# Block sums of the turned rows, made in two halves behind later reciprocal roots: a decoder layer on one core

## The chip, the cores and the metric

The kernel runs on one core of a Trainium2 chip. The metric is the device time of one execution in microseconds (us). The engines are TensorE (PE), VectorE (DVE), ScalarE (ACT), GpSimd (POOL) and SyncE (SP), whose queue issues the DMAs.

## The reference

One layer of a hybrid decoder over a prompt of 2048 rows and 64 sample rows, all in float32 and 1024 wide: input projection, windowed attention and a pooling mixer, an output projection, an MLP of width 4096, and a gate. What matters here stands in the middle:

```
  mix = concat(RMSNorm(attn), RMSNorm(pool)) @ w_out
  x  += RMSNorm(mix)
  x  += RMSNorm(relu(RMSNorm(x) @ w_up)^2 @ w_down)
```

The first row's product and residual, the norm of the new x, and its turning into the operand of `@ w_up` are the place of the change.

## The kernel before, in words

The rows are 16 tiles of 128 (t = 0 to 15) and one of the 64 sample rows (t = -1); two tiles make a pair, pair p having the tiles 2p and 2p + 1. Products are made in three matmuls for accuracy: each operand is split into a rounded half (a cast on ScalarE, L214) and a rest (a subtraction on VectorE, L137).

The stages, by the trace: input projection, attention and pooling until about 425 us; the output mixing until about 600; the up projection until about 1290; the down projection until about 1910; then the gate. The up projection multiplies in blocks of 2 x 2 with seven products instead of eight. Of the turned rows it needs four blocks A11, A12, A21, A22 (the halves of an even tile and of an odd one) as the seven operands A11, A12, A22, S1 to S4, where

    s0 = A21 + A22, s1 = s0 - A11, s2 = A11 - A21, s3 = A12 - s1

are S1 to S4. The kernel writes the operands of every pair to three scratch blocks in DRAM (`hfd`), and the up projection reads them back one block of 352 columns at a time (`sp<-hfd`, L1041; A22 by L1272).

The output mixing goes over the tiles 0, 1, 2, 3, -1, 4, 5 and so on to 13. For a tile:

- `Mixed.product` (L245 to L264) does the products into PSUM (`pab`, L141 to L143) and takes them out: the first half by ScalarE (L260), the second by VectorE with an addition (L262), into `z`.
- `first_residual` (L921 to L932) does the residual: a sum of squares of z on ScalarE (L190, `junk`), a reciprocal root on GpSimd (`rstd_of`: L148 `rst`, then L150 `rsq`), L927 and L928 on VectorE (the new x, stored by L929), a second sum of squares (L190, `z`), a second root, and L931, the normed rows.
- `turned` (L934 to L945) turns the rows of the tile two before: eight transposes on TensorE (L941, `trx`), two copies on ScalarE (L944) into `h`, of which there are three buffers.
- `operands` (L947 to L956) runs behind the odd tile of a pair: four sums by GpSimd (`a_sums`, L898 to L902: L899 s0, L900 s1, L901 s2, L902 s3) into `s`, two buffers; then the stores to `hfd` (L956), from `h` and from `s`.

Pair 7 (tiles 14, 15) is late: its residual and turning run inside the first rounds of the up projection, and `space` makes its operands. Weights of the up projection come in by L1144 (`raw`), are split (`g`), and PSUM is copied out by L1198 (`snap`).

The kernel's instructions are placed by a scheduler that takes each engine's order from the program's order, priorities and its own estimates. `tc.issue_after(x)` tells it to issue what follows on the engine behind x. All loads and stores named here go in one order through SyncE's queue, so one that waits holds all behind it.

Of the kernel before, what the change touches and what calls it, by code (L numbers as in the profile page):

```python
# [14 lines left out]
ALU = mybir.AluOpType  # L15
# [17 lines left out]
NT = SEQ // P  # L33
# [62 lines left out]
def trunk(ctx: ExitStack, tc: tile.TileContext, i: dict, o: dict):  # L96
    nc = tc.nc
    V, A, G, T, SY = nc.vector, nc.scalar, nc.gpsimd, nc.tensor, nc.sync
# [25 lines left out]
    ones, mhalf = small[:, 0:1], small[:, 1:2]  # L124
# [14 lines left out]
    def mm3(ps, lhs, rhs, first, last):  # L139
# [2 lines left out]
        T.matmul(ps, lhs[0], rhs[1], start=False, stop=False)  # L142
        T.matmul(ps, lhs[1], rhs[0], start=False, stop=last)  # L143

    def rstd_of(pool, ss, n, dim, cols=1):

        r = pool.tile([P, cols], F32, tag="rst", bufs=6, name="rst")
        G.tensor_scalar(out=r[:n], in0=ss, scalar1=1.0 / dim, scalar2=EPS, op0=ALU.mult, op1=ALU.add)  # L148
        q = pool.tile([P, cols], F32, tag="rsq", bufs=6, name="rsq")
        G.tensor_tensor(out=q[:n], in0=r[:n], in1=mhalf[:n].to_broadcast([n, cols]) if cols > 1 else mhalf[:n], op=ALU.pow)  # L150
        return q

    def pool(stack, name, bufs=1, **k):
# [5 lines left out]
    class Ring:  # L159
# [11 lines left out]
        def first(self, k):  # L171

            n = len(self.slots)
            self.more(k)
            at = self.n % n
            self.slots, self.n = self.slots[n:] + self.slots[at:n] + self.slots[:at], 0
# [105 lines left out]
    with ExitStack() as sa:  # L282
# [8 lines left out]
        op = sa.enter_context(tc.tile_pool(name="op", bufs=2, space=PSUM, reuse_waits="tile"))  # L291
# [533 lines left out]
        first = front(-1, *heads[-1], res[-1])  # L825
# [5 lines left out]
        for t in range(-1, NT):  # L831
# [8 lines left out]
            p = pooling(t, u, mix, sq)  # L840
# [24 lines left out]
    with ExitStack() as sb:  # L865
# [10 lines left out]
        def pieces(tp):  # L876

            at = tp * P if tp >= 0 else NT // 2 * P
            end, out = at + wid(tp), []
            c = at  # L880
            while c < end:
                n = min(end, (c // UP_N + 1) * UP_N) - c
                out.append((c // UP_N, c % UP_N, c - at, n))
                c += n
            return out
# [9 lines left out]
        pld = {tp: [dp.tile([P, 2, 512], F32, name=f"pld{tp + 1}{k}") for k in range(2)] for tp in range(-1, NT // 2)}  # L895
        zd = {tp: dp.tile([P, 2, D], F32, name=f"zd{tp}") for tp in SPILLED}

        def a_sums(eng, s, a11, a12, a21, a22):  # L898
            eng.tensor_tensor(out=s[:, 0], in0=a21, in1=a22, op=ALU.add)  # L899
            eng.tensor_tensor(out=s[:, 1], in0=s[:, 0], in1=a11, op=ALU.subtract)  # L900
            eng.tensor_tensor(out=s[:, 2], in0=a11, in1=a21, op=ALU.subtract)  # L901
            eng.tensor_tensor(out=s[:, 3], in0=a12, in1=s[:, 1], op=ALU.subtract)  # L902

# [1 line left out]
        with s2:  # L907
            p2 = pool(s2r, "p2", side="right")
            gpost, gmlp = rows_of(p2, "g_post_mix"), rows_of(p2, "g_pre_mlp")

            def mix_out(t, nh):
                if t not in mixed.z:
                    mixed.z[t] = p2.tile([P, D], F32, tag="z", bufs=2, name="z")
                    mixed.load(t)
                for _ in mixed.product(t, nh, acc, p2):
                    pass

            added = {}

            def first_residual(t):  # L920

                n = tn(t)
                z = mixed.z[t]
                xt = p2.tile([P, D], F32, tag="xt", bufs=2, name="xt")
                SY.dma_start(xt[:n], xrows(t))
                rs = sumsq(p2, z[:n], n, p2.tile([P, D], BF16, tag="junk", bufs=1, name="junk"))
                V.scalar_tensor_tensor(out=z[:n], in0=z[:n], scalar=rs[:n], in1=gpost[:n], op0=ALU.mult, op1=ALU.mult)  # L927
                added[t] = V.tensor_tensor(out=xt[:n], in0=xt[:n], in1=z[:n], op=ALU.add)  # L928
                SY.dma_start(x1d[t][:n], xt[:n])  # L929
                rs = sumsq(p2, xt[:n], n, z)  # L930
                V.scalar_tensor_tensor(out=z[:n], in0=xt[:n], scalar=rs[:n], in1=gmlp[:n], op0=ALU.mult, op1=ALU.mult)  # L931
                return z  # L932

            def turned(t, z, after=False):  # L934

                n = tn(t)
                h8 = p2.tile([P, 8, P], F32, tag="h", bufs=3, name="h")
                for j in range(2):
                    ps = trb.tile([P, 4, P], F32, tag="tr", name="trx")
                    for c in range(4):  # L940
                        m = T.transpose(ps[:, c, :n], z[:n, (4 * j + c) * P : (4 * j + c + 1) * P], ident[:n, :n])  # L941
                        if after and c == 0:
                            tc.keep_in_program_order(m)
                    A.copy(out=h8[:, 4 * j : 4 * j + 4, :n], in_=ps[:, :, :n])  # L944
                return h8  # L945

            def operands(tp, a, b):  # L947

                n = wid(tp)
                (a11, a12), (a21, a22) = halves(a), halves(b)  # L950
                s = p2.tile([P, 4, 4, P], F32, tag="s", bufs=2, name="s")[:, :, :, :n]
                a_sums(G, s, a11, a12, a21, a22)
                for blk, off, c0, m in pieces(tp):
                    for k, src in ((A11, a), (A22, a22), (S1, s.rearrange("p s c n -> p (s c) n"))):
                        dst = hfd[blk][:, k : k + src.shape[1] // 4, :, off : off + m].rearrange("p o c n -> p (o c) n")
                        SY.dma_start(dst, src[:, :, c0 : c0 + m])  # L956

            h8 = {}

            def turn(t):  # L960

                h8[t] = turned(t, normed.pop(t), True)
                if t < 0:
                    operands(-1, h8[t][:, :, : NS // 2], h8[t][:, :, NS // 2 : NS])
                elif t % 2:
                    operands(t // 2, h8[t - 1], h8[t])

            normed, due = {}, []
            for tp in [0, 1, -1, 2, 3, 4, 5, 6]:
                for t in pairs_of(tp):  # L970
                    if tp:
                        mix_out(t, 0)
                        mix_out(t, 1)
                        if len(due) > 1 or due[0] > 1:
                            turn(due.pop(0))
                    normed[t] = first_residual(t)
                    due.append(t)


            late = list(pairs_of(NT // 2 - 1))  # L980
            for nh in range(2):
                for t in late:
                    mix_out(t, nh)
                    while due:
                        turn(due.pop(0))
            late_h = []

            def turn_late():
                t = late[len(late_h)]
                late_h.append(turned(t, normed[t], True))  # L990

            def residual_late(k):
                normed[late[k]] = first_residual(late[k])
# [22 lines left out]
        with ExitStack() as s3:  # L1016
# [32 lines left out]

            def space():  # L1050

                operands(NT // 2 - 1, *late_h)
                s2r.close()
                for n in ("x0", "x1"):
                    ops[n] = Ring(s3, n, 1)
                g3.first(3)
# [912 lines left out]
```

## Time and profile before

| | us |
|---|---|
| median of 3 runs | 2132.93 |
| the runs | 2132.93, 2133.65, 2127.79 |
| profiled execution, its own time | 2133.05 |
| span of the profiled execution | 2131.2 |
| granted TensorE clock, mean | 0.996 |

The span is from the first instruction to the last; 1.85 us of the time lie around it. In rows of the timeline the first number is the start in us, the second the duration in us, then engine, line, operation, output <- input, shapes, and in brackets how long the engine was idle before and what ended it. The four sums of a pair on GpSimd, in one view that groups the rows of 420 to 640 us by line (pair -1's smaller ones among them, "+1 forms"):

```profile
L901 POOL TENSOR_TENSOR s<-h 128x512 f32<-128x512 f32 (+1 forms) x9 | 17.0, 1890 | 13.5 <-ACT h L944 13.5
L900 POOL TENSOR_TENSOR s<-s,h 128x512 f32<-128x512 f32 (+1 forms) x9 | 16.9, 1879 | 0.7
L899 POOL TENSOR_TENSOR s<-h 128x512 f32<-128x512 f32 (+1 forms) x9 | 16.8, 1872 | 0.6 <-ACT h L944 0.6
L902 POOL TENSOR_TENSOR s<-h,s 128x512 f32<-128x512 f32 (+1 forms) x9 | 11.9, 1326 | 0.6
```

Behind the bar stand the busy time, the mean ns of one, and the idle time of GpSimd just before them with what ended it: 62.6 us of sums in all.

### The profile page before, as it was taken

How to read it: one execution, taken by the hardware profiler on the slowest of the kernel's cores; microseconds unless marked ns; L12 is line 12 of the kernel's file. 1: busy time of each engine (PE TensorE's matmuls, PEld its weight loads, DVE VectorE, ACT ScalarE, POOL GpSimd, SP SyncE). 2: the span in 40 equal slices, each digit the busy share in tenths (PEclk: the TensorE clock that was granted, in tenths of full speed). 3: DMA queues.
4: the chain of work that ended last, by engine and by line, in shares of the span. 5: the costliest groups of instructions: out<-in, count | busy, mean ns of one | idle time of the engine just before them, and what ended most of it. 6: DMA issues, size and time to landing. Idle time of an engine off the chain costs nothing.

```text
span 2131.2 us, 31320 instructions
## 1 busy us (share of the span) xinstructions
PE 2099.9 (99%) x11223; PEld 1851.0 (87%) x11223; DVE 1609.5 (76%) x2749; ACT 1029.7 (48%) x2018; POOL 646.9 (30%) x689
## 2 busy tenths in 40 slices
PE   9999999999999999999999999999999999999999
PEld 7888888788789999999999998888888888887787
DVE  6888988776689888655654567778888888896786
ACT  4667676645455456454544445523323323333553
POOL 1434444354441110000000004643443443432242
PEclk9999999999999999999999999999999999999999
DMA  7453322768789989986767663223123123248563
GB/s 221 147 175 97 93 63 91 268 217 248 226 252 320 310 288 348 273 246 204 233 207 217 213 191 113 80 93 121 51 92 100 51 92 101 90 159 333 187 196 121
DMA packets 334250, 379.76 MB, mean 178 GB/s; under 512 B 82511, under 2 KB 263951, under 8 KB 323822
## 3 DMA queue, kind: packets, MB, share of 16 engines
q1 hardware_dynamic: 334094, 377.76, 55.5%
q8 instruction: 88, 1.44, 0.3%
q14 instruction: 68, 0.56, 0.1%
HBM read 247.90 MB, written 131.09 MB: 178 GB/s over the span
## 4 chain that ended last, share of the span: by engine, by line
PE 78%; DMA 6%; DVE 6%; issue 4%; POOL 3%; ACT 2%; SPq 1%; DVEq 0%; ACTq 0%; POOLq 0%
PE dn L1483 10%; PE dn L1485 10%; PE dn L1484 10%; PE up L1191 9%; PE up L1193 9%; PE up L1192 9%; PE pg L1720 2%; PE pg L1722 2%; PE pg L1721 2%; PE trp L584 1%; PE qps L141 1%; PE qps L143 1%; PE qps L142 1%; DMA x<-in_x_prompt_dram 1%; DMA xt<-in_x_t_dram 1%
## 5 line engine op out<-in xcount | busy, mean ns | idle before, releaser
L1493 DVE TENSOR_TENSOR z<-dn,z 128x512 f32<-128x512 f32 x416 | 280.0, 685 | 91.5 <-PE dn L1485 85.3
L137 DVE TENSOR_TENSOR g<-raw,g 128x512 fp32r<-128x512 f32 x336 | 233.6, 713 | 98.6 <-ACT g L214 91.1
L1191 PE MATMUL up<-e,g 128*128 128x352 f32 x832 | 268.4, 324 | 5.1 <-ACT snap L1198 4.7
L1192 PE MATMUL up<-e,g 128*128 128x352 f32 x832 | 268.0, 322 | 0.0
L1193 PE MATMUL up<-e,g 128*128 128x352 f32 x832 | 265.0, 323 | 0.0
L214 ACT CAST g<-raw 128x512 fp32r<-128x512 f32 x336 | 203.4, 622 | 87.0 <-PE up L1193 64.6
L1432 POOL TENSOR_TENSOR raws<-raws 128x1024 f32<-128x1024 f32 x32 | 80.3, 2511 | 429.0 <-DMA raws<-in_w_down_dram 376.0
L1483 PE MATMUL dn<-wr,ms 128*128 128x512 f32 x512 | 199.4, 390 | 0.0
L1484 PE MATMUL dn<-wr,ms 128*128 128x512 f32 x512 | 199.2, 389 | 0.0
L1485 PE MATMUL dn<-wr,ms 128*128 128x512 f32 x512 | 198.0, 389 | 0.0
L1191 PEld LDWEIGHTS up<-e,g 128*128 128x128 f32 x832 | 156.6, 188 | 6.9 <-ACT snap L1198 5.3
L1192 PEld LDWEIGHTS up<-e,g 128*128 128x128 f32 x832 | 157.3, 189 | 0.7
L1193 PEld LDWEIGHTS up<-e,g 128*128 128x128 f32 x832 | 156.1, 188 | 0.0
L214 ACT CAST m<-fr 128x512 fp32r<-128x512 f32 (+1 forms) x128 | 65.4, 515 | 182.5 <-PE dn L1485 156.6
L899 POOL TENSOR_TENSOR s<-fr 128x256 f32<-128x256 f32 x64 | 49.1, 767 | 332.2 <-DVE ms L137 241.8
L1483 PE MATMUL dn<-wr,m 128*128 128x512 f32 x384 | 149.7, 390 | 0.0
L1484 PE MATMUL dn<-wr,m 128*128 128x512 f32 x384 | 149.4, 389 | 0.0
L1485 PE MATMUL dn<-wr,m 128*128 128x512 f32 x384 | 149.4, 389 | 0.0
L1205 DVE TENSOR_TENSOR t<-up,snap 128x352 f32<-128x352 f32 x144 | 71.3, 520 | 77.3 <-ACT snap L1198 66.1
L1198 ACT COPY snap<-up 128x352 f32<-128x352 f32 x144 | 62.2, 454 | 136.8 <-PE up L1193 136.8
L1483 PEld LDWEIGHTS dn<-wr,ms 128*128 128x128 f32 x512 | 96.1, 188 | 20.4 <-DVE z L1493 0.4
L1485 PEld LDWEIGHTS dn<-wr,ms 128*128 128x128 f32 x512 | 96.1, 188 | 20.0
(398 smaller groups left out, 5772.9 us busy)
## 6 DMA issues: line engine op xcount, KB each, us to landing
raw<-in_w_up_dram SPq DMA_DIRECT2D x160, 256.0 KB, 4.9
raw<-upt SPq DMA_DIRECT2D x32, 1024.0 KB, 8.0
fr<-ffd SPq DMA_DIRECT2D x64, 512.0 KB, 3.6
ffd<-r SPq DMA_DIRECT2D x96, 256.0 KB, 3.0
upt<-raw SPq DMA_DIRECT2D x16, 1024.0 KB, 5.8
raws<-in_w_down_dram SPq DMA_DIRECT2D x32, 512.0 KB, 5.3
sp<-hfd SPq DMA_DIRECT2D x21, 704.0 KB, 5.6
gwd<-gw SPq DMA_DIRECT2D x28, 512.0 KB, 5.9
```

What stands on the lines that cost most here:

```text
L137: eng.tensor_tensor(out=out, in0=full, in1=hi.bitcast(F32), op=ALU.subtract)
L214: copy(out=dst[:, 0], in_=src)
L1191: T.matmul(ps, l[0], r[0], start=st, stop=False, skip_group_check=not fresh)
L1192: T.matmul(ps, l[0], r[1], start=False, stop=False, skip_group_check=not fresh)
L1193: T.matmul(ps, l[1], r[0], start=False, stop=c == 3, skip_group_check=not fresh)
L1198: snapped.append(A.copy(out=s, in_=ps))
L1205: V.tensor_tensor(out=t, in0=ps, in1=s, op=ALU.add)
L1432: tc.keep_in_program_order(G.tensor_tensor(out=t, in0=x, in1=y, op=ALU.subtract))
L1483: T.matmul(ps, l[0], r[0], start=fresh and j == 0, stop=False, skip_group_check=not fresh)
L1484: T.matmul(ps, l[0], r[1], start=False, stop=False, skip_group_check=not fresh)
L1485: T.matmul(ps, l[1], r[0], start=False, stop=j == 1, skip_group_check=not fresh)
L1493: V.tensor_tensor(out=z, in0=ps, in1=z, op=ALU.add)
```

## The change

`rstd_of` remembers its latest root in `rooted`. `a_sums` takes a part: 0 makes s0 and s2, 1 makes s1 and s3, none all four. `operands` stores A11, A12 and A22 at once and puts the two halves of the sums into a list; the second half also stores S1 to S4. A new `gap`, called at the end of each `first_residual`, takes one half off the list and issues it behind the latest root, which is that tile's second. So a pair's halves lie behind the second roots of two successive tiles. For pair 7, `space` empties the list at once.

```diff
+    rooted = [None]
...
-        G.tensor_tensor(out=q[:n], in0=r[:n], in1=mhalf[:n].to_broadcast([n, cols]) if cols > 1 else mhalf[:n], op=ALU.pow)
+        rooted[0] = G.tensor_tensor(out=q[:n], in0=r[:n], in1=mhalf[:n].to_broadcast([n, cols]) if cols > 1 else mhalf[:n], op=ALU.pow)
...
-        def a_sums(eng, s, a11, a12, a21, a22):
-            eng.tensor_tensor(out=s[:, 0], in0=a21, in1=a22, op=ALU.add)
-            eng.tensor_tensor(out=s[:, 1], in0=s[:, 0], in1=a11, op=ALU.subtract)
-            eng.tensor_tensor(out=s[:, 2], in0=a11, in1=a21, op=ALU.subtract)
-            eng.tensor_tensor(out=s[:, 3], in0=a12, in1=s[:, 1], op=ALU.subtract)
+        def a_sums(eng, s, a11, a12, a21, a22, part=None):
+            if part != 1:
+                eng.tensor_tensor(out=s[:, 0], in0=a21, in1=a22, op=ALU.add)
+                eng.tensor_tensor(out=s[:, 2], in0=a11, in1=a21, op=ALU.subtract)
+            if part != 0:
+                eng.tensor_tensor(out=s[:, 1], in0=s[:, 0], in1=a11, op=ALU.subtract)
+                eng.tensor_tensor(out=s[:, 3], in0=a12, in1=s[:, 1], op=ALU.subtract)
...
                 V.scalar_tensor_tensor(out=z[:n], in0=xt[:n], scalar=rs[:n], in1=gmlp[:n], op0=ALU.mult, op1=ALU.mult)
+                gap()
                 return z
...
-                a_sums(G, s, a11, a12, a21, a22)
-                for blk, off, c0, m in pieces(tp):
-                    for k, src in ((A11, a), (A22, a22), (S1, s.rearrange("p s c n -> p (s c) n"))):
-                        dst = hfd[blk][:, k : k + src.shape[1] // 4, :, off : off + m].rearrange("p o c n -> p (o c) n")
-                        SY.dma_start(dst, src[:, :, c0 : c0 + m])
+
+                def store(*srcs):
+                    for blk, off, c0, m in pieces(tp):
+                        for k, src in srcs:
+                            dst = hfd[blk][:, k : k + src.shape[1] // 4, :, off : off + m].rearrange("p o c n -> p (o c) n")
+                            SY.dma_start(dst, src[:, :, c0 : c0 + m])
+
+                def first():
+                    a_sums(G, s, a11, a12, a21, a22, 0)
+
+                def second():
+                    a_sums(G, s, a11, a12, a21, a22, 1)
+                    store((S1, s.rearrange("p s c n -> p (s c) n")))
+
+                store((A11, a), (A22, a22))
+                sums.extend((first, second))
+                if now:
+                    while sums:
+                        sums.pop(0)()
+
+            sums = []
+
+            def gap():
+
+                if sums:
+                    with tc.issue_after(rooted[0].ins):
+                        sums.pop(0)()
...
-                operands(NT // 2 - 1, *late_h)
+                operands(NT // 2 - 1, *late_h, now=True)
```

The lines of the changed kernel are numbered two higher from L143 on, and more behind `a_sums`: L150 and L152 are the root, L902, L903, L905, L906 are s0, s2, s1, s3, L949 the copies to `h`, L962 the stores to `hfd`, L1068 the operand loads, L1171 the weights, L1225 `snap`.

**GpSimd, the sums of pair 3** (tiles 6 and 7; `s_6237` before, `s_6233` after). Before, from the second root of tile 8:

```order
L150 TENSOR_TENSOR rsq_6159<-rst_6157,small_69 128x1
L901 TENSOR_TENSOR s_6237<-h_6130,h_6224 128x512
L899 TENSOR_TENSOR s_6237<-h_6224 128x512
L900 TENSOR_TENSOR s_6237<-s_6237,h_6130 128x512
L148 TENSOR_SCALAR rst_6250<-ss_6248 128x1
L902 TENSOR_TENSOR s_6237<-h_6130,s_6237 128x512
L150 TENSOR_TENSOR rsq_6252<-rst_6250,small_69 128x1
```

Now, from the second root of tile 10:

```order
L152 TENSOR_TENSOR rsq_6350<-rst_6348,small_69 128x1
L902 TENSOR_TENSOR s_6233<-h_6220 128x512
L903 TENSOR_TENSOR s_6233<-h_6124,h_6220 128x512
L150 TENSOR_SCALAR rst_6438<-ss_6436 128x1
L152 TENSOR_TENSOR rsq_6440<-rst_6438,small_69 128x1
L150 TENSOR_SCALAR rst_6447<-ss_6445 128x1
L152 TENSOR_TENSOR rsq_6449<-rst_6447,small_69 128x1
L905 TENSOR_TENSOR s_6233<-s_6233,h_6124 128x512
L906 TENSOR_TENSOR s_6233<-h_6124,s_6233 128x512
```

The four sums, which stood around tile 9's first root, are now two behind tile 10's second root and two behind tile 11's.

**ScalarE, the end of the mixing and the entry of the up projection.** `z_6659` is tile 14's z before, `z_6653` now; `junk_7080` and `junk_7071` are tile 15's first sum of squares; `l0` is the cast of S4. Before:

```order
L944 COPY h_6706<-trx_6707 128x512
L260 ACTIVATE z_6727<-pab_6733,rap_67 128x512
L260 ACTIVATE z_6727<-pab_6789,rap_67 128x512
L944 COPY h_6706<-trx_6713 128x512
L190 ACTIVATE z_6659,ss_7015<-xt_7003 128x1024
L214 CAST l0_6944<-sp_6942 128x1408
L190 ACTIVATE junk_7080,ss_7081<-z_6727 128x1024
L1198 COPY snap_6968<-up_6955 128x352
```

Now:

```order
L262 ACTIVATE z_6716<-pab_6722,rap_67 128x512
L262 ACTIVATE z_6716<-pab_6778,rap_67 128x512
L192 ACTIVATE z_6653,ss_7004<-xt_6992 128x1024
L192 ACTIVATE junk_7071,ss_7072<-z_6716 128x1024
L216 CAST l0_6933<-sp_6931 128x1408
L1225 COPY snap_6957<-up_6944 128x352
L216 CAST l1_6975<-sp_6936 128x1408
L216 CAST g3_7018<-raw_6939 128x512
L949 COPY h_6700<-trx_6701 128x512
L949 COPY h_6700<-trx_6707 128x512
```

Tile 13's copies to `h` stood around the two L260; they are now behind the first `snap`. Tile 15's junk is now ahead of the cast of S4.

**SyncE, the same place.** `sp_6942` before and `sp_6931` now are the load of S4 for the up projection's first block. Before:

```order
L956 DMA hfd1_5253<-s_6629 128x16x64
L956 DMA hfd2_5254<-s_6629 128x16x64
L956 DMA hfd2_5254<-h_6693 128x8x128
L929 DMA x1d14_5294<-xt_6640 128x1024
L1144 DMA raw_7098<-in_w_up_dram 128x4x128 x2
L925 DMA xt_7078<-in_x_prompt_dram 128x1024
L1144 DMA raw_7098<-in_w_up_dram 128x4x128 x2
L1041 DMA sp_6942<-hfd0_5252 128x1408
```

Now:

```order
L933 DMA x1d14_5294<-xt_6631 128x1024
L929 DMA xt_7069<-in_x_prompt_dram 128x1024
L962 DMA hfd1_5253<-s_6430 128x16x128
L962 DMA hfd2_5254<-h_6687 128x8x128
L1171 DMA raw_7093<-in_w_up_dram 128x4x128 x4
L1068 DMA sp_6931<-hfd0_5252 128x1408
```

Ahead of the weights and the load of S4 stood the sums of pair 5 (`s_6629`); now those of pair 4 (`s_6430`) stand there, and pair 5's store has gone into the up projection, ahead of the weights of its fourth round.

More of the change, by code (lines that the diff above doesn't have):

```diff
@@ L945, in turned, with operands @@
                 return h8
-            def operands(tp, a, b):
+            def operands(tp, a, b, now=False):
                 n = wid(tp)
```

## The prediction

> **What bounds the kernel now.** I read the page first: busy times, then the costliest groups.
>
> ```profile
> PE 2099.9 (99%) x11223; PEld 1851.0 (87%) x11223; DVE 1609.5 (76%) x2749; ACT 1029.7 (48%) x2018; POOL 646.9 (30%) x689
> L1191 PE MATMUL up<-e,g 128*128 128x352 f32 x832 | 268.4, 324 | 5.1 <-ACT snap L1198 4.7
> ```
>
> TensorE is busy for 2099.9 of 2131.2 us. The change takes no matmul away, so all it can give back is time in which TensorE waits or runs slowly near the moved sums. The first sum is made soon after 420 us and the last before 640; so the second view is TensorE's own waits from 420 to 700 us.
>
> ```profile
> PE up L1191 <- ACT snap L1198: 4.1, 1, 4.1
> PE pab L141 <- ACT z L260: 1.3, 1, 1.3
> PE up L1191 <- ACT g L214: 0.4, 1, 0.4
> ```
>
> Columns: total us, times, longest. Two waits matter. The timeline of TensorE has them (start, duration, and in brackets the idle time before):
>
> ```profile
> 567.96 0.39 PE L143 MATMUL pab<-wo,ms 128*128 128x512 f32 x1
> 569.69 0.50 PE L141 MATMUL pab<-wo,ms 128*128 128x512 f32 x1 [1.34 <-ACT z L260]
> ...
> 605.60 0.32 PE L1193 MATMUL up<-e,g 128*128 128x352 f32 x1
> 610.07 0.43 PE L1191 MATMUL up<-e,g 128*128 128x352 f32 x1 [4.14 <-ACT snap L1198]
> ...
> 610.74 0.50 PE L1191 MATMUL up<-e,g 128*128 128x352 f32 x1
> 611.03 0.50 PE L1192 MATMUL up<-e,g 128*128 128x352 f32 x1
> ```
>
> The first is inside the output mixing (L141 to L143): start to start 1.73 us where a matmul takes about 0.23, so 1.5 lost. The second is at the entry of the up projection: 4.47 from start to start, 4.3 lost. Behind it 11 matmuls start 0.29 apart (610.74 to 611.03) where I count 0.16 before and after: another 11 x 0.13 = 1.5 us at a lower clock. With two smaller gaps of about 0.5 us together that I found between matmul starts, and 0.4 from the table, the sum of everything the change could win is 1.5 + 4.3 + 1.5 + 0.5 + 0.4 = 8.2 us, 0.4% of the run. That is the first bound.
>
> A rule of the Trainium skill bears on the slow matmuls: "TensorE: Matmul & The Clock Gate", Part 1, says that an idle window of some 3.4 us halves the clock until the engine has been busy for as long. The trace agrees in part: the 4.14 us wait is followed by about 3 us at 0.29 against 0.16. By this rule the 1.5 us go as soon as the wait falls clearly below 3.4 us; my forecast does not need it.
>
> **Why the sums could matter at all: the loop of the residual.** Each tile of the mixing has two sums of squares; GpSimd makes a reciprocal root of each (L148, L150), VectorE then scales (L927, L931), corrects the next operand (L137) and adds the next products (L262), after which ScalarE's next sum of squares (L190) starts the next tile. So first root to first root is the length of one turn. GpSimd's timeline, a pair with its four block sums:
>
> ```profile
> 487.48 0.19 POOL L148 TENSOR_SCALAR rst<-ss 128x1 f32<-128x1 f32 x1 [0.59 <-ACT junk L190]
> ...
> 498.15 0.19 POOL L148 TENSOR_SCALAR rst<-ss 128x1 f32<-128x1 f32 x1 [5.11 <-ACT junk L190]
> ...
> 523.25 0.25 POOL L148 TENSOR_SCALAR rst<-ss 128x1 f32<-128x1 f32 x1 [5.11 <-ACT junk L190]
> ...
> 529.46 1.89 POOL L901 TENSOR_TENSOR s<-h 128x512 f32<-128x512 f32 x1 [0.59 <-ACT h L944]
> 531.30 2.28 POOL L899 TENSOR_TENSOR s<-h 128x512 f32<-128x512 f32 x1
> 533.66 2.77 POOL L900 TENSOR_TENSOR s<-s,h 128x512 f32<-128x512 f32 x1
> 536.51 0.19 POOL L148 TENSOR_SCALAR rst<-ss 128x1 f32<-128x1 f32 x1
> 536.78 1.29 POOL L902 TENSOR_TENSOR s<-h,s 128x512 f32<-128x512 f32 x1
> ...
> 548.51 0.25 POOL L148 TENSOR_SCALAR rst<-ss 128x1 f32<-128x1 f32 x1 [5.11 <-ACT junk L190]
> ```
>
> A turn without a sum takes 498.15 - 487.48 = 10.67 us. With sums 536.51 - 523.25 = 13.26, then 548.51 - 536.51 = 12.00: 12.63 on the mean. TensorE's own pace comes from the grouped rows of 60 us without a wait:
>
> ```profile
> L141 PE MATMUL pab<-wo,ms 128*128 128x512 f32 x82 | 32.5, 396 | 0.0
> L941 PE MATMUL trx<-ident,z 128*128 128x128 f32 x40 | 5.2, 272 | 0.0
> ```
>
> 82 of L141 in 60 us, and 16 to a tile: 60 x 16 / 82 = 11.7 us a tile. The loop with sums (12.63) is 0.9 slower than TensorE, the loop without (10.67) faster by 1.0; TensorE begins with a lead and uses it up at about 544 us, and only then waits. That is the 1.5 us at 568.
>
> **What the change does to the loop.** It adds and removes no instruction on GpSimd: two sums behind the second root of each of two tiles instead of four in a row behind the turned odd tile. Two effects oppose each other.
>
> *Gain.* L900 stands no more ahead of a first root (533.66 to 536.43, the root at 536.51), nor L902 between the two halves of one (1.29 us). The dear turn loses up to 13.26 - 12.00 = 1.3 us, so 0.6 us a tile at most if the cheap one stays as it is.
>
> *Loss.* VectorE's L931 waits for that same second root, so the sums now start at the same moment as L931 and L137, on every tile. What that does is in VectorE's rows beside a pair's sums and away from them:
>
> ```profile
> 599.66 2.31 DVE L927 SCALAR_TENSOR_TENSOR z<-z,rsq,g_post_mix 128x1024 f32<-128x1024 f32 x1 [2.19 <-POOL rsq L150]
> 602.00 2.20 DVE L928 TENSOR_TENSOR xt<-xt,z 128x1024 f32<-128x1024 f32 x1
> ...
> 612.45 1.27 DVE L927 SCALAR_TENSOR_TENSOR z<-z,rsq,g_post_mix 128x1024 f32<-128x1024 f32 x1
> ```
>
> ```profile
> 591.92 2.33 POOL L148 TENSOR_SCALAR rst<-ss 128x1 f32<-128x1 f32 x1 [4.45 <-ACT z L190]
> ...
> 599.59 1.30 POOL L901 TENSOR_TENSOR s<-h 128x512 f32<-128x512 f32 x1
> 600.91 2.21 POOL L899 TENSOR_TENSOR s<-h 128x512 f32<-128x512 f32 x1
> ```
>
> The same L927 takes 2.31 where a sum started 0.07 us earlier, and 1.27 alone; the second sum takes 2.21 instead of 1.30. They take turns. Placed behind the second root: sum one 0 to 1.3 us, L931 done at 2.3 (instead of 1.3), sum two to 3.5, L137 to 4.6 (instead of 2.5), the two L262 to 6.0. So the path is longer by up to 2 us than the turn without a sum: 10.67 + 2.0 = 12.7 us, on every tile. Against 12.63 that is nothing. If VectorE went first, the turn would be about 1 us shorter, 11.7, which is TensorE's own pace.
>
> The Trainium skill's "SBUF — State Buffer", section on the two separate sides, says that VectorE operations with two SBUF inputs and GpSimd share a port pair under an exclusive lock, and that whoever starts first keeps it for the whole instruction. The rows above agree (2.31 against 1.27). By the rule the order of arrival decides, and it speaks against this change: GpSimd, whose own root has just ended, would arrive first.
>
> The h copies (L944) come into this too. Their buffers (three) come free only behind the sums, which are now behind the previous tile's second root. ScalarE therefore makes them behind the products' copies L260, as the rows in the section on the change show. That takes the first half's copy (about 0.6 us) out of the way of L260, for which TensorE waited at 569.69; at 3.5 us behind the root the sums end before L262 does (6.0), so the copies hide beside VectorE. I take the mixing as even: bounds are -2.0 us (1.5 and the small gaps vanish) and, if every turn costs the dear 13.26, (13.26 - 12.63) x 9 tiles with full sums = +5.7.
>
> **The entry of the up projection.** ScalarE's rows:
>
> ```profile
> 604.30 1.06 ACT L190 ACTIVATE z<-xt 128x1024 f32<-128x1024 f32 x1 [3.46 <-DVE xt L928]
> ...
> 607.26 1.37 ACT L214 CAST l<-sp 128x1408 fp32r<-128x1408 f32 x1 [1.81 <-DMA sp<-hfd]
> 608.53 1.05 ACT L190 ACTIVATE junk<-z 128x1024 bf16<-128x1024 f32 x1
> ...
> 609.58 0.43 ACT L1198 COPY snap<-up 128x352 f32<-128x352 f32 x1
> ```
>
> The copy of PSUM (L1198) that TensorE waits for since 605.9 stands behind the cast l, and that behind a DMA of the operand S4. In the changed order the 1.05 us of junk stand ahead of the cast, in time spent waiting for the DMA: if the DMA lands at 607.2 as before, the copy comes at 608.5, a gain of 1.05. What sets the landing is on SyncE's queue:
>
> ```profile
> 586.99 1.59 SPq L956 DMA_DIRECT2D hfd<-s  x2
> ...
> 596.84 0.93 SPq L1144 DMA_DIRECT2D raw<-in_w_up_dram  x2
> ...
> 599.43 0.46 SPq L1041 DMA_DIRECT2D sp<-hfd  x1
> ```
>
> The load stands behind four weight loads (raw), which wait for VectorE's last L137 on the previous weights. Two things come new ahead of it. The S store of 1 MB for pair 4 (s_6430 in the order) waits for the second half of its sums behind tile 13's second root: its L148 ends at 594.25 above (591.92 + 2.33, held up beside VectorE), plus 2.6 for two sums alone, 3.5 beside VectorE, so 597 to 598. And VectorE's L137 contend with these sums. So S4 leaves at 599 to 601 and lands, with 1 MB more ahead of it, up to 3.3 us later. The price of 1 MB is from the windows (DMA share and GB/s last):
>
> ```profile
> 570.00:600.00 30.00, 29.98 (x144) 24.70 (x143) 19.25 (x22) 16.55 (x31) 12.88 (x15) 1.00 0.66 169
> 600.00:612.00 12.00, 7.86 (x45) 7.57 (x44) 8.83 (x8) 6.53 (x10) 8.34 (x8) 0.94 0.96 302
> 612.00:640.00 28.00, 28.00 (x176) 27.96 (x175) 25.43 (x36) 15.18 (x31) 10.44 (x6) 0.96 0.83 261
> 640.00:700.00 60.00, 59.55 (x371) 58.94 (x370) 56.28 (x92) 32.25 (x62) 6.31 (x4) 1.00 1.01 325
> ```
>
> At 302 GB/s 1 MB is 3.5 us. From zero to 3.5 late against 1.05 gained: -1 to +2.5, and below that -5.8 (4.3 + 1.5) if S4 is early because the raw weights come free earlier. I take -0.5, near the end with no delay, since the 30 us ahead move only 169 GB/s and have room for a store.
>
> Later stores: pair 5's 1 MB of S goes from 587 into the time behind tile 15's second root, about 624. There the DMA engines have a few idle microseconds (the window from 612 to 640 has a share of 0.83); from 640 on they are full (1.01), and a store that is not done by then costs up to 3.3 us (1 MB at 325 GB/s) of the weight stream. The weights have some slack behind 630, so I take nothing. Everything after the up projection's first block has the same order on all engines: nothing.
>
> **Sum.** Mixing 0, entry -0.5, later 0: about 2132.5 from the profiled 2133.05 (span 2131.2 plus 1.85 around it). The median of the runs, 2132.93, is 0.1 below that, so the forecast on its scale is **2132**.
>
> **Rivals.** (1) *The loop falls to TensorE's pace.* VectorE gets its turn first, the turns are 11.7, TensorE reaches the entry late by nothing, z(14) is early since pair 6's sums no longer stand beside L927 and L928 (2.31 and 2.20 instead of 1.27), and S4 with it: -2.0 - 5.8 = -7.8 at most, 2125; half of it 2129. For it: GpSimd is idle for 5.11 us ahead of the first roots. Against: the sums start at the root, not in that idle time, and S4 does not hang on z(14). (2) *Every turn becomes a dear one*, because sum two, the late S3 cast's L137 (in one tile between L931 and the next) and the h copies follow one another on every tile: +5.7, plus a slow entry with 1 to 2.5: 2139 to 2141. Decides from turns of 13.2 us on. For it: the port is shared at the worst place. Against: first roots are no longer held by L900. (3) *S4 lands late*, mixing even: +2.5 to +3.3, 2135 to 2136. That the sums are not moved at all is excluded by the order itself.
>
> **How the numbers follow.** About even, 2130 to 2135: 0.50. Rival 1: 0.22, half of it with over 6.4 us. Rival 2: 0.16. Rival 3: 0.12. A measurement of this kernel can tell about 0.3% (6.4 us) from no change; the three runs before lie 5.9 apart. Faster by more: 0.11; slower by more: 0.17 (rival 2 and a little of rival 3); within: 0.72. The range runs from 2126 to 2140: rival 1 but for its best end, rival 2's nearer part.
>
> **What would show it.** Turns between first roots of 12.5 to 12.9 on all tiles, instead of 13.2 and 12.0 in turn, would show the loop right; L931 at 2.3 and L137 at about 2.2 beside a sum would show the contention. The wait at the entry should stay between 3 and 5.5 us with the slow matmuls behind it. The forecast is wrong if turns are 11.7 or below, if the cast l starts before 605 or after 610, or if TensorE gets waits of over 1 us between 612 and 700.

## The result, and the profile after

The changed kernel takes **2147.41 us** (median of 6 runs, 2142.76 to 2151.55) against 2131.29 (6 runs, 2127.79 to 2133.65): slower, ratio 1.0076, 95% interval 1.0064 to 1.0089. The forecast was 2132 with a range to 2140. The profiled execution is the fastest of the six: 2142.76, span 2141.0, 9.8 us above the span before. Of the 16 us between the medians the two profiles show 10: the profiled execution before is 1.8 above its median, and the changed kernel's median is 4.7 above its profiled one. What slower executions lose more is in no profile; a second profile of the same kernel, further down, has a time of 2144.32.

TensorE's work is nearly the same. The page's first line and the group that carried the wait before:

```profile
PE 2105.1 (98%) x11223; PEld 1855.3 (87%) x11223; DVE 1626.1 (76%) x2749; ACT 1032.4 (48%) x2018; POOL 641.7 (30%) x689
L1218 PE MATMUL up<-e,g 128*128 128x352 f32 x832 | 268.5, 324 | 3.9 <-ACT snap L1225 3.9
```

What grew is TensorE's waits from 420 to 760 us (total, times, longest):

```profile
PE pab L141 <- ACT z L262: 5.3, 2, 4.6
PE up L1218 <- ACT snap L1225: 4.8, 2, 3.4
PE pab L143 <- DVE ms L137: 2.5, 1, 2.5
PE up L1220 <- DVE g L137: 2.0, 2, 1.4
```

They add up to 14.6 us, against 7.0 before in the same window (the waits shown ahead and one of 1.0 for snap behind 700). The wait in the mixing (the first and third row) has gone from 1.3 to 7.8; the entry's wait for snap has fallen from 4.1 to 3.4, and 2.0 for weights are new. The timeline of TensorE has the two in the mixing:

```profile
566.25 0.39 PE L143 MATMUL pab<-wo,ms 128*128 128x512 f32 x1
571.22 0.80 PE L141 MATMUL pab<-wo,ms 128*128 128x512 f32 x1 [4.59 <-ACT z L262]
...
586.24 0.39 PE L142 MATMUL pab<-wo,ms 128*128 128x512 f32 x1
589.10 0.50 PE L143 MATMUL pab<-wo,ms 128*128 128x512 f32 x1 [2.47 <-DVE ms L137]
```

Behind the first, matmuls start 0.43 apart instead of 0.23 until 576.5 (granted clock 0.50 from 573 to 576), which is 2.5 us more; behind the second wait it is about 1.1. The 1.5 us of slow matmuls behind the entry are still there, 0.29 apart from 617.8 to 620.8. So there are 7.6 more of waits and 3.6 more of slow matmuls.

The rows of TensorE can also be counted by stage, since both traces have all of them. From the first to the last of the 800 matmuls of the mixing's products (`pab`) it is 204.4 us before and 214.7 now, so the mixing takes 10.3 more. The first 200 matmuls of the up projection take 39.7 and 41.7. From the first product of the mixing to the end of the span it is 12.0 more; the spans differ by less, 9.8, because this execution came to the mixing 2.3 us earlier.

**The loop did what the prediction worked out, and one thing more.** GpSimd's timeline of the changed kernel (first roots are the rst that a junk released):

```profile
535.61 0.19 POOL L150 TENSOR_SCALAR rst<-ss 128x1 f32<-128x1 f32 x1 [3.68 <-ACT junk L192]
...
541.08 1.29 POOL L905 TENSOR_TENSOR s<-s,h 128x512 f32<-128x512 f32 x1
542.45 2.16 POOL L906 TENSOR_TENSOR s<-h,s 128x512 f32<-128x512 f32 x1
548.28 0.19 POOL L150 TENSOR_SCALAR rst<-ss 128x1 f32<-128x1 f32 x1 [3.68 <-ACT junk L192]
...
561.91 0.57 POOL L150 TENSOR_SCALAR rst<-ss 128x1 f32<-128x1 f32 x1 [4.56 <-ACT junk L192]
...
576.45 0.19 POOL L150 TENSOR_SCALAR rst<-ss 128x1 f32<-128x1 f32 x1 [5.21 <-ACT junk L192]
...
584.47 1.29 POOL L902 TENSOR_TENSOR s<-h 128x512 f32<-128x512 f32 x1
...
591.64 0.19 POOL L150 TENSOR_SCALAR rst<-ss 128x1 f32<-128x1 f32 x1 [3.67 <-ACT junk L192]
```

548.28 - 535.61 = 12.67 us for a turn, as worked out; the one before it took 13.05. The next three are 13.63, 14.54 and 15.19. Why they grow stands in ScalarE's and VectorE's rows:

```profile
568.27 1.37 ACT L216 CAST e<-sp 128x1408 fp32r<-128x1408 f32 x1 [1.39 <-DMA sp<-hfd]
569.54 1.04 ACT L216 CAST ms<-mr 128x1024 fp32r<-128x1024 f32 x1
570.49 1.26 ACT L262 ACTIVATE z<-pab,rap 128x512 f32<-128x512 f32 x2
...
580.78 1.38 ACT L216 CAST e<-sp 128x1408 fp32r<-128x1408 f32 x1 [4.42 <-DMA sp<-hfd]
582.07 1.05 ACT L192 ACTIVATE z<-xt 128x1024 f32<-128x1024 f32 x1
```

```profile
567.83 2.28 DVE L935 SCALAR_TENSOR_TENSOR z<-xt,rsq,g_pre_mlp 128x1024 f32<-128x1024 f32 x1 [2.14 <-POOL rsq L152]
570.03 2.69 DVE L137 TENSOR_TENSOR e<-sp,e 128x1408 fp32r<-128x1408 f32 x1
572.64 1.22 DVE L137 TENSOR_TENSOR ms<-mr,ms 128x1024 fp32r<-128x1024 f32 x1
...
584.54 2.30 DVE L935 SCALAR_TENSOR_TENSOR z<-xt,rsq,g_pre_mlp 128x1024 f32<-128x1024 f32 x1 [0.72 <-POOL rsq L152]
586.77 2.28 DVE L137 TENSOR_TENSOR ms<-mr,ms 128x1024 fp32r<-128x1024 f32 x1
```

The casts e are the S operands of the up projection's first block, S3 at 568.27 and S1 at 580.78. ScalarE does its work in order, so while it waits for their DMA everything behind it waits: at 568.27 the cast of ms and the L262 for which TensorE stands still, at 580.78 the second sum of squares of the loop. The second wait, for ms, ends with L137 at 589.05: that L137 and the L935 ahead of it run beside sums of pair 4 and take 2.3 each.

The loads are late because a store of the sums is, and because they follow one another through one buffer. SyncE's queue:

```profile
544.64 3.08 SPq L962 DMA_DIRECT2D hfd<-s  x2
...
551.38 0.52 SPq L1068 DMA_DIRECT2D sp<-hfd  x1
...
562.46 0.32 SPq L1068 DMA_DIRECT2D sp<-hfd  x1
...
571.26 0.37 SPq L962 DMA_DIRECT2D hfd<-s  x1
572.75 1.77 SPq L1068 DMA_DIRECT2D sp<-hfd  x1
```

The store at 544.64 is that of pair 2's sums, part of which the first block reads. Behind it S2's load leaves at 551.38, where it left at 523.48 before. S3's load leaves when VectorE has ended with S2's rest, at 562.46. The load of S1 stands behind the store of pair 3's sums, which before was issued at 538.10, but what it waits for last is the buffer: it leaves at 572.75, as soon as VectorE has ended with S3's rest (570.03 + 2.69), and lands eight us later.

The collision itself, in groups of VectorE from 420 to 600 us, L931 before and L935 now:

```profile
L931 DVE SCALAR_TENSOR_TENSOR z<-xt,rsq,g_pre_mlp 128x1024 f32<-128x1024 f32 (+1 forms) x13 | 17.7, 1363 | 19.2 <-ACT ms L214 15.6 <-POOL rsq L150 3.7
```

```profile
L935 DVE SCALAR_TENSOR_TENSOR z<-xt,rsq,g_pre_mlp 128x1024 f32<-128x1024 f32 (+1 forms) x13 | 27.3, 2099 | 19.3 <-ACT ms L216 10.8 <-POOL rsq L152 8.4
```

17.7 has become 27.3 us for the same 13 instructions. The rule of the Trainium skill ("SBUF — State Buffer", the section on the two separate sides) that the prediction weighed, that whoever comes first keeps the shared ports for the whole instruction, is what the rows of the changed kernel show: GpSimd's first sum takes 1.29, L935 beside it 2.3.

### The profile page after: what moved, and what is told of

The parts are those of the page before. It is cut to its first block, busy times and chain, and to the rows that moved or that the text cites. A ratio compares the mean times of both kernels' runs of the same rounds, so it can differ in the third digit from the quotient of the medians.

```text
span 2141.0 us, 31293 instructions
## 1 busy us (share of the span) xinstructions
PE 2105.1 (98%) x11223; PEld 1855.3 (87%) x11223; DVE 1626.1 (76%) x2749; ACT 1032.4 (48%) x2018; POOL 641.7 (30%) x689
## 4 chain that ended last, share of the span: by engine, by line
PE 75%; DMA 7%; DVE 6%; issue 6%; POOL 3%; ACT 2%; SPq 1%; DVEq 0%; ACTq 0%; POOLq 0%
PE dn L1510 9%; PE dn L1512 9%; PE dn L1511 9%; PE up L1220 8%; PE up L1218 8%; PE up L1219 8%; PE pg L1747 2%; PE pg L1749 2%; PE pg L1748 2%; DMA gwd<-gw 1%; PE trp L586 1%; DMA wod<-wsp 1%; PE qps L141 1%; PE qps L143 1%; PE qps L142 1%
## 5 line engine op out<-in xcount | busy, mean ns | idle before, releaser
L137 DVE TENSOR_TENSOR g<-raw,g 128x512 fp32r<-128x512 f32 x336 | 241.4, 738 | 91.0 <-ACT g L216 84.9
L902 POOL TENSOR_TENSOR s<-fr 128x256 f32<-128x256 f32 x64 | 49.1, 767 | 332.7 <-DVE ms L137 245.5
L1225 ACT COPY snap<-up 128x352 f32<-128x352 f32 x144 | 62.2, 455 | 129.7 <-PE up L1220 129.7
```

The source lines that it names most:

```text
L137: eng.tensor_tensor(out=out, in0=full, in1=hi.bitcast(F32), op=ALU.subtract)
L1225: snapped.append(A.copy(out=s, in_=ps))
```

## The experiments

All are shown against runs of the kernel before on the same chip.

| run | halves behind second roots | median us | ratio, 95% interval |
|---|---|---|---|
| the change | up to pair 5; pair 6 when `space` empties the list | 2147.41 | 1.0076 [1.0064, 1.0089] |
| e1 | pairs 3 to 6 | 2138.59 | 1.0035 [1.0022, 1.0048] |
| e2 | 0 to 2, the rest at once | 2134.11 | 1.0015 [1.0006, 1.0025] |
| e3 | as the change, casts of S2, S3, S1 later | 2145.24 | 1.0064 [1.0049, 1.0079] |
| e4 | as the change, behind VectorE's L137 up to tile 12 | 2131.64 | 1.0000 [0.9990, 1.0010] |
| e5 | pairs 3 and 4 | 2131.85 | 1.0014 [1.0005, 1.0023] |
| e6 | pairs 0 to 4 | 2138.27 | 1.0040 [1.0025, 1.0054] |
| e7 | none | 2130.16 | 1.0002 [0.9992, 1.0011] |
| e8 | as e4, a tile earlier | 2140.60 | 1.0052 [1.0037, 1.0067] |
| e9 | as e8, pairs 0 to 4 | 2138.22 | 1.0036 [1.0024, 1.0047] |
| e10 | kernel before, snap ahead of S4's cast | 2133.45 | 1.0011 [1.0001, 1.0020] |
| e11 | e9 and e10 together | 2140.28 | 1.0049 [1.0030, 1.0068] |
| e12 | the change again | 2145.63 | 1.0070 [1.0049, 1.0092] |
| e13 | pairs 5 and 6 as in the change, the rest at once | 2139.43 | 1.0051 [1.0034, 1.0068] |
| e14 | 0 to 2 exactly as in the change | 2138.10 | 1.0052 [1.0034, 1.0071] |
| e15 | as e14, behind L137 | 2135.42 | 1.0025 [1.0015, 1.0035] |

The edits move the scheduler's order on other engines, too, so a run is never one price alone. Each run has one profile, of one execution.

**e1: pairs 0 to 2 at once.**

```diff
-                if now:
+                if now or tp < 3:
```

> Only pairs 3 to 5 have their halves behind the second roots; pairs 0, 1, -1 and 2, which make up the first block of the up projection, have them at once as before. Theory A (the late S operands of the first block: their casts stand in ScalarE's and VectorE's order ahead of the residual's steps and wait for DMA, which holds the mixing at 566 to 593 us): the loss goes, 2128 to 2135 us, no TensorE wait over 2 us between 540 and 600. Theory B (sums and VectorE colliding behind every second root): tiles 10 to 13 still collide, 2138 to 2145.

Measured 2138.59, by the time in theory B's range. But in the mixing theory A holds: no wait over 0.8 us from 540 to 600, where the change has 7.1. The time is not back, since two waits of 4.8 us stand behind it, one of them new, in the up projection:

```profile
638.72 0.52 PE L1218 MATMUL up<-l,g 128*128 128x352 f32 x1 [4.73 <-DVE t L1232]
```

GpSimd runs eight sums on end there, pair 6's and pair 7's:

```profile
624.37 1.29 POOL L902 TENSOR_TENSOR s<-h 128x512 f32<-128x512 f32 x1
...
636.25 1.59 POOL L906 TENSOR_TENSOR s<-h,s 128x512 f32<-128x512 f32 x1
```

So there are two places, not one. (The list is shorter in this run, so it is pair 6 and not pair 5 that the gap behind tile 15's root took. The expectation counts pair -1 to the first block; its 32 columns are in the third, by `pieces`.)

**e2: the reverse.**

```diff
-                if now:
+                if now or tp > 2:
```

> The reverse: only pairs 0, 1, -1, 2 have their halves behind the second roots, pairs 3 to 5 at once. Theory A: the first block's S operands are as late as in the change, so 2141 to 2149, with waits at 565 to 595 as there. Theory B: half the collisions are gone, 2134 to 2140.

Measured 2134.11, which speaks against theory A. But the run is weaker than meant: pair 3 at once empties the list, and so pulled pair 2's second half forward. e14 does it properly.

**e3: the casts of S2, S3 and S1 later.**

```diff
-{k: mixed.taken[PIN0 + j, 1] for j, k in enumerate(OPS[:5])}
+{k: mixed.taken[(7, 8, 11, 13, 14)[j], 1] for j, k in enumerate(OPS[:5])}
```

> The change, but the casts of S3 and S1 for the first block are held behind the takings-out of tiles 13 and 14 instead of 10 and 11, so they no longer stand ahead of tile 11's and 12's residual. Theory A: the waits at 566 to 593 (4.7 and 2.6 us and the slow matmuls behind them, about 11 together) go, 2133 to 2138; the entry at 614 may wait 1 to 3 us more. Theory B: 2144 to 2149, as the change.

Measured 2145.24, in theory B's range. The wait at 566 falls from 4.6 to 0.8 us, the one at 584 is now 3.2 us, and between 615 and 628 there are four waits of 1.4 to 3.3. Holding the casts back moves their price to the entry: the loads stay late. (The edit also moves S2's cast, from behind tile 9's taking-out to behind tile 11's.) The turns at tiles 11 and 12 are 12.88 and 12.63 again, but the mixing's products still take 211.4 us, 7.0 more than before: the wait of 3.2 is for ms, whose L137 runs beside a sum.

**e4: no collision up to tile 12.** A dependence on VectorE's L137 behind the second root holds each half back; its core is:

```diff
+                for x in held_back.pop(places.index(t) - 3, ()):
+                    tc.add_manual_dep(x.ins, y.ins.name, mybir.DependencyInfo(mybir.DependencyClass.Sync, mybir.DependencyReason.DATA), reason="gap")
```

> The change, but each half of the sums also waits for VectorE's L137 that follows L931 of the same tile, so the two engines no longer collide there. Theory A: turns between first roots fall from 12.7 to about 10.7 or TensorE's own 11.7, but the S operands are as late or 2 us later and their casts still hold tiles 11 and 12: 2136 to 2147. Theory B: 2124 to 2132.

Measured 2131.64, in theory B's range and the time of before. GpSimd's order is that of the change; the sums up to tile 12 now stand in the idle time ahead of the first root. The halves behind the second roots of tiles 13 to 15 have no such L137 to wait for and collide as in the change (at 587.44, 598.69 and 616.77). Ahead of the first root:

```profile
551.06 1.29 POOL L906 TENSOR_TENSOR s<-h 128x512 f32<-128x512 f32 x1 [2.53 <-DVE ms L137]
552.31 1.29 POOL L907 TENSOR_TENSOR s<-h 128x512 f32<-128x512 f32 x1
553.68 0.19 POOL L152 TENSOR_SCALAR rst<-ss 128x1 f32<-128x1 f32 x1
...
565.37 0.67 POOL L152 TENSOR_SCALAR rst<-ss 128x1 f32<-128x1 f32 x1 [0.86 <-ACT junk L194]
...
579.29 0.19 POOL L152 TENSOR_SCALAR rst<-ss 128x1 f32<-128x1 f32 x1
```

Both sums take 1.29, the turn before 553.68 took 10.7 us (from 543.02). The turns with late casts are still long, 11.7 and 13.9, but TensorE now has the lead to cover them: no wait in the mixing at all, whose products take 202.1 us, 2.3 less than before. All its waits from 420 to 700 are these:

```profile
PE up L1225 <- ACT g L218: 4.0, 2, 2.0
PE up L1227 <- DVE g L137: 2.8, 2, 1.8
```

The mixing's gain is given back there: TensorE starts the up projection at 595.4 instead of 600.0 (half of this lies ahead of the mixing), and waits for weights, beside pair 6's sums from 604.5 to 612.3. Its first 200 matmuls take 44.6 us instead of 39.7.

**e5: pairs 3 and 4 alone.**

```diff
-                if now:
+                if now or tp not in (3, 4):
```

> Only pairs 3 and 4 have their halves behind the second roots; unlike the run with pairs 3 to 5, pair 5's sums are made at once, before the up projection. Theory C (in that run the loss of 7 us came from pair 5's and 6's eight sums, which ran from 624 to 638 beside VectorE's work for the up projection): 2129 to 2134, no TensorE wait of over 3 us between 615 and 660. If the loss came from the collisions in the mixing: 2136 to 2140.

Measured 2131.85, as theory C said. Four colliding turns with the first block's operands on time cost little (1.0014); the mixing's products take 205.2 us, 0.8 more than before.

**e6: pairs 5 and 6 at once.**

```diff
-                if now:
+                if now or tp > 4:
```

> The change, but pair 5's sums (and the rest of pair 4's) are made at once, not behind tile 14's and 15's second roots. Theory C: the loss in the mixing (10 us at 566 to 593) stays, what the change loses behind 615 goes: 2137 to 2143. If all of the change's loss is in the mixing: 2145 to 2149. If all is behind it: 2129 to 2134.

Measured 2138.27, in theory C's range: the mixing waits as in the change,

```profile
PE pab L141 <- ACT z L262: 4.9, 2, 4.1
PE pab L143 <- DVE ms L137: 3.0, 1, 3.0
```

and 8 us of the 16 remain. The mixing's products take 214.1 us, 9.7 more than before; the first 200 matmuls of the up projection take 39.4, as before. (The edit makes pair 6's sums at once too.)

**e7: halves, no delay.**

```diff
-                if now:
+                if True:
```

> The halves without any delay: A11, A12 and A22 stored at once and the sums in the order s0, s2, s1, s3, but all four of them when the odd tile is turned, as before. All theories: 2128 to 2134, no difference; outside of it the order of the parts or of the stores has a price of its own.

Measured 2130.16, no difference. Neither the new order of the four sums nor the early stores of A11, A12 and A22 have a price.

**e8: no collision, and a tile earlier.**

```diff
-                sums.extend((first, second))
+                sums.extend([lambda: first() + second()] if tp < 0 else (first, second))
```

on top of e4.

> Each half waits for VectorE's L137 behind the second root (no collision), and pair -1's small sums go behind one root, so that all later halves stand one tile earlier than in the change. Theory C: turns of 10.7 in the mixing with the late casts taken in by the lead, S operands 10 us earlier, pair 5's sums before the up projection: 2122 to 2129. If the collisions are not what takes the lead: 2131 to 2140.

Measured 2140.6, outside both ranges: the mixing waits 1.1 us only, but at the entry and at 633.7 the same two waits as in e1 come, 4.9 and 4.7. With the list one entry shorter pair 6's sums go behind tile 15's second root again.

**e9: e8 with pairs 5 and 6 at once.**

```diff
-                if now:
+                if now or tp > 4:
```

> The last run with pairs 5 and 6 made at once again: only pairs 0 to 4 are in halves, each waiting for VectorE's L137. Theory C (what that run lost came from pair 6's four sums, which stood behind tile 15's second root and ran with pair 7's beside VectorE from 624 to 638): 2125 to 2132, no wait of over 3 us behind 615. If its loss is the price of the waits on VectorE in the mixing: 2136 to 2142.

Measured 2138.22, outside theory C's range. It is in the other one, but the mixing's products take 204.6 us, so the loss is not there. The wait at 633.7 is gone, as expected, but smaller ones stand from 613 to 671: 2.0 for VectorE's rests of the weights, 1.6 for ScalarE's casts of them, 1.2 for VectorE's t. Theory C explains e8 by one wait; this run shows that the first rounds of the up projection lose several us in more than one way. What in the new order did it here is not settled.

**e10: snap ahead of S4's cast, in the kernel before.**

```diff
-                o7s[0].update(load_ops(0, OPS[5:6]))
+                s4 = sp3.tile([P, 4, UP_N], F32)
+                SY.dma_start(s4, hfd[0][:, S4])
```

and S4 is split where A22 is, behind the first snap.

> The kernel before with one edit: the cast of S4 for the first block stands behind the first copy of PSUM (snap) on ScalarE instead of ahead of it. If the entry's wait of 4.1 us is the cast waiting for its DMA: the wait falls below 2 us and the slow matmuls behind it go, 2124 to 2129. If the next weights (raw) are as late, the wait moves on to them: 2128 to 2132.

Measured 2133.45: the wait moves on. TensorE's rows at the entry:

```profile
605.36 0.43 PE L1191 MATMUL up<-e,g 128*128 128x352 f32 x1 [1.35 <-ACT snap L1198]
...
608.97 0.43 PE L1191 MATMUL up<-e,g 128*128 128x352 f32 x1 [1.28 <-ACT g L214]
...
611.41 0.66 PE L1191 MATMUL up<-e,g 128*128 128x352 f32 x1 [1.85 <-ACT g L214]
```

1.35 + 1.28 + 1.85 = 4.5 in place of 4.1. The snap was not the only bound: behind it ScalarE's casts of the weights (g) wait for their DMA, until 610.74, and TensorE with them. So the 5.8 us that the prediction offered rival 1 at the entry were not to be had from this side.

**e11: both.** The edits of e9 and e10.

> Both edits of the two runs before together: pairs 0 to 4 in halves behind VectorE's L137, and snap ahead of the cast of S4. If the mixing's gain (about 2 us) and the entry's (up to 5.8) add up: 2121 to 2127. If the mixing's gain only becomes a longer wait for the weights at the entry: the same time as the run before.

Measured 2140.28: the gains do not add up, and no version beat the kernel before.

**e12: the change again.**

> The changed kernel once more, for a second profile: its six runs lay from 2142.8 to 2151.6, and the one profile is of the fastest. Theory C: the places of the loss are the same (565 to 593 and 613 to 660), and a slower run loses more at these places; otherwise the rest of the loss is at a place not yet looked at.

Measured 2144.32 and 2146.94, a profile of the first. It waits at the same places: 5.0 for z and 3.0 for ms in the mixing, 2.2 for snap, 1.9 and 0.9 for weights. The expectation's second part stays untested, as the slowest executions have no profile.

**e13: pairs 5 and 6, where the change has them.**

```diff
-                sums.extend((first, second))
-                if now:
+                sums.extend((first, second) if tp != 5 else (lambda: None, first, second))
+                if now or tp < 5:
```

> Only pair 5 is in halves, behind tile 14's and 15's second roots as in the change; all other pairs at once as before, so the mixing is that of before. Theory D (the change loses in two places that are independent: about 8 in the mixing and 7 to 9 by pair 5's sums in the up projection's first rounds): 2136 to 2140. If pair 5's place only costs when the mixing is late too: 2129 to 2133.

Measured 2139.43, in theory D's range. Pair 6 is not made at once either: its halves stay on the list until `space` empties it, as in the change. The mixing is that of before (one wait of 1.3 us, 204.0 us for its products). At the entry S4 comes sooner and the wait for snap is 0.8, but two waits for weights, 2.5 and 3.4, take its place. The longer one:

```profile
614.18 0.66 PE L1220 MATMUL up<-e,g 128*128 128x352 f32 x1 [3.42 <-DVE g L137]
```

```profile
607.92 2.31 POOL L903 TENSOR_TENSOR s<-h 128x512 f32<-128x512 f32 x1
...
613.65 1.61 POOL L906 TENSOR_TENSOR s<-h,s 128x512 f32<-128x512 f32 x1
```

```profile
610.70 1.75 DVE L1179 TENSOR_TENSOR raw<-raw 128x512 f32<-128x512 f32 x1
612.38 1.75 DVE L137 TENSOR_TENSOR g<-raw,g 128x512 fp32r<-128x512 f32 x1
```

Tile 13's copies to h wait for pair 5's first half, so pair 6's four sums come late and on end, from 607.9 to 615.3, beside the two operations on the weights that TensorE needs next. Those take 1.75 instead of 0.68. The first 200 matmuls of the up projection take 44.1 us here, 4.4 more than before, and slow matmuls are part of it. From the first product of the mixing to the end this execution takes 8.5 more, so 4 us of the loss come later, 3.3 of them behind 800 us; why is not settled.

**e14 and e15: the first block exactly as late as in the change, with collisions and without.**

```diff
-                sums.extend((first, second))
+                if now or tp < 3:
+                    sums.extend((first, second))
+                else:
+                    first()
+                    second()
```

e15 is the same on top of e4.

> Pairs 0, 1, -1 and 2 exactly as in the change (pair 2's second half behind tile 9's second root, which the earlier run of this kind did not hold), pairs 3 to 5 at once: the first block's S operands are as late as in the change and six of its halves collide. If lateness is what costs: 2137 to 2141; if it costs only where every later turn is 12.7 us too: 2130 to 2135.

> The same, but the halves of pairs 0, 1, -1 and 2 also wait for VectorE's L137: the S operands as late, without collisions in the delayed halves. If collisions are what costs: 2128 to 2133; if lateness: 2136 to 2141.

Measured 2138.1 and 2135.42, the second between what the two theories gave. The operands are late in both (in e15 the casts of S2, S3 and S1 start at 560.1, 569.3 and 578.1, about as in the change). The profiles put the losses in different places. In e14, whose profile is of its fastest execution, 2133.85, the mixing's products take 208.8 us, 4.4 more than before. In e15 they take 204.6, and the loss comes behind the entry: 4.3 us between the 200th and the 400th matmul of the up projection, with a wait of 1.3 for snap and one of 2.0 for weights. So late operands whose halves do not collide cost nothing in the mixing; what e15 loses later is not explained.

## Why the prediction was wrong, point by point

- **What bounds the kernel, and the most that could be won (8.2 us).** Held: no run was clearly faster than before. The bound says nothing on what can be lost.
- **"The turn is 12.7 us, on every tile."** Right up to tile 10 (13.05 and 12.67 in the last two turns before it), and L935 (L931 before) at 2.3 and L137 at 2.3 beside a sum as worked out. But from tile 10 on turns were 13.6, 14.5 and 15.2.
- **"I take the mixing as even."** This is the step that failed first. The term was 0, at most +5.7; the change's profile has +10.3 for the mixing's products, e12's 11.4 and e6's 9.7. A mean turn as long as before was taken to mean as much waiting as before. Two things were charged nothing. Within a turn, the prediction itself has L137 end at 4.6 us behind the root instead of 2.5, and TensorE waits for that ms: e3, with the late casts out of the way and turns of 12.6 to 12.9, still loses 7.0. And it was not worked out where the S operands' casts stand. They come from stores that are moved with the sums, and I followed the stores to S4 and the weights only. The casts on ScalarE and VectorE are ahead of the residual's own steps in order, so a late load holds the loop. Rival 2 named the late S3 cast's L137, but not the wait of 4.42 us for S1's DMA.
- **Collisions and lateness.** The prediction weighed the collision alone, and found it to be neutral. The time of the mixing's products, 204.4 us before, sorts the runs. With collisions in the turns from tile 9 on and the operands on time it is 204.7 and 205.2 (e1, e5). With late operands and no collision of the delayed halves it is 204.6 (e15), and with all halves up to tile 12 held it is 202.1 (e4). With both it is 208.8 (e14, pairs 0 to 2) and 214.1 to 215.8 (e6, the change, e12); with the late casts out of the way, still 211.4 (e3). So late operands alone cost the mixing nothing and a few collisions little; by e3, collisions behind all second roots cost most of the 10 us, and the late casts the rest. In e4 turns of 10.7 us give TensorE the lead that takes in the late casts; with 12.7 there is none. I read it so, though the runs differ in other engines' order as well, and no run has collisions behind every second root with the operands on time; e3 comes nearest.
- **The entry, -0.5.** The wait there did fall (4.1 to 3.4) and the cast of S4 was late as feared (its row starts at 615.59, which missed the stated 610), but TensorE was late as well. The prediction expected the slow matmuls to go once the wait is clearly below 3.4 us; they also follow the wait of 2.47 us in the mixing.
- **"Later 0."** The second step that failed. TensorE has waits of 1.4 and 0.7 us for weights at 625.2 and 629.6 in the change. The prediction looked at the store of pair 5's sums (issued at 636.44, not at 624). What it left out is the sums themselves: pair 5's first half holds the buffer that tile 13's copies need, those hold pair 6's sums, and these then run beside VectorE's weights. e13, with the mixing of before, is 9.2 us above before by its median; in its profile the first 200 matmuls of the up projection lose 4.4. In the change's two profiles they lose less, 1.9 and 1.4. The order rows shown ahead of the prediction have tile 13's copies behind snap; the step to pair 6 was not taken.
- **Rivals.** Rival 2 (slower) is the nearest in kind, with 0.16. Its turns of 13.2 us and more came from tile 10 on, but by late loads, not on every tile; its price was 2139 to 2141. Rival 1 did not come, and e10 shows that its price at the entry was not to be had. Rival 3's late S4 came (its cast starts at 615.59 instead of 607.26), but TensorE was late by as much.

e6 (8.3 us over the runs of before beside it) and e13 (9.2) add up to 17.5, near the change's 16.1, and either alone would have left the forecast's even case. That the two places are independent is not shown, though. e4 has pairs 5 and 6 as in the change and takes the time of before, and the change's own profiles lose nearly all in the mixing. What the change loses beyond what these profiles show, and where, stays open.

## What to carry to other kernels

When a step is moved, follow its results to their last reader: a DMA that leaves later is a cast that waits later, and in an engine's fixed order that wait falls on whatever stands behind it. A buffer that is released later also moves the work that fills it, and that can end up beside the one stage that has no idle time. And an idle gap on an engine is only used by work that starts in it: here the gap lay behind VectorE's work, not behind the root (e4).

## What the runs showed of the hardware that was not expected

Taking turns costs a VectorE operation about the same whatever its own length: the normed rows (L935) go from 1.28 to 2.31, the rest of an operand from 1.63 to 2.69, and an operation on the weights from 0.68 to 1.75 (610.70 and 612.38 in e13), 1.03 to 1.07 us each, beside sums that take 1.3 alone. So the short operations lose most in proportion. And slow matmuls came behind a wait of 2.47 us (589.10 in the change): from 591.3 to 593.5 they start 0.43 apart, and the granted clock from 591 to 593 is 0.50. Behind the wait of 1.37 at 625.20 they did not come.
